# A transformer block on one Trainium2 core: other orders of operations at the edges of the two feed-forward blocks, and the last norm's weight taken into the last scaling

## The chip, the cores and the metric

The kernel runs on 1 core of one Trainium2 chip. The metric is the device time of one execution in microseconds (us). The core's engines work side by side, each through its own queue of instructions strictly in the order in which the program issues them: PE (TensorE, matmuls and transposes), DVE (VectorE), ACT (ScalarE), POOL (GpSimd) and SP (SyncE, which only starts transfers here). An instruction waits at the head of its queue until what it reads is there, and all behind it on that engine wait with it.

## The reference, cut

One block with fp32 weights and rows x of 512 x 1024, feed-forward width 2816:

```python
h = rms_norm(x, norm_ffn1);  x = x + 0.5 * swiglu(h, ffn1_gate, ffn1_up, ffn1_down)
h = rms_norm(x, norm_mix)    # RWKV7 time mix and sliding window attention on h @ w_in -> mixed
x = x + mixed @ w_out
h = rms_norm(x, norm_ffn2);  x = x + 0.5 * swiglu(h, ffn2_gate, ffn2_up, ffn2_down)
return rms_norm(x, norm_final)

def rms_norm(x, g):
    return x * rsqrt(mean(x * x, axis=-1) + 1e-5) * g
def swiglu(x, wg, wu, wd):
    return (silu(x @ wg) * (x @ wu)) @ wd
```

## The kernel before

Every fp32 product is made of three matmuls of rounded parts (`mm3w`, L679): high x high, low x high, high x low. So each operand exists as a high and a low part. ACT makes the high part by a copy (`high`, L160, names hia, hib for the weights of block a and b; L583 for the activations), DVE the low part by subtracting it (`low`, L169, loa and lob; L584).

The program has four stages: feed-forward block a, the mixer, `out_mix` (the product with w_out and its residual add), feed-forward block b with the final norm behind it. Names end in a or b by block.

A feed-forward block (`ffn`, L589) walks through *pieces* q of its weights, 128 x 1024 each, which `Stream` loads into rings of raw tiles (rawa0, rawa1, rawb), in the main on SP's queue; some pieces are sums of two blocks of weights, and for these POOL issues a second transfer that adds to the first (L128). Pieces 0 to 3 are *plain*: `plain_step` multiplies them with the block's operands into four accumulators Pa or Pb, one for each row tile t, six matmuls for each. Pieces 4 to 73 belong to a scheme of seven products for every 2 x 2 blocks, in the order M1 M2 M7 M6 M5 M3 M4 (accumulators X, Q, Y); M7 takes the difference s3 of two turned operands (L556). The 22 pieces after them are the down product, for the column half h = 0 and then h = 1. Step q of `ffn` issues, in this order: the loads of later pieces, the split of piece q + 2 (high and low part), the high part of piece q + 3, then `early` (work on operands), then the step of piece q itself, and last the *hidden turns* that are due, transposes of the gated values gta or gtb to hta or htb (L729).

The operands come from *turns*: `operand_turn` (L542) transposes four 128 x 128 blocks of row tile t, half h on PE into PSUM (xta, xtb; two such tiles exist), and DVE multiplies them by the norm's gain into xga or xgb (L549). `operand_split` then makes the two parts (ACT L583, DVE L584) into operands AaM, AaP (AbM, AbP). The norm's row scales do not enter the operands. They come from `row_squares` (ACT, L403, one square for each row tile) and `row_scales` (DVE L412, a pow on POOL into ms L414, DVE L416), and are first used by the gate gta, gtb (L656 on ACT, L657 on DVE).

In block a, `plain_step` of piece 0 turns rows 2 and 3 between its accumulators t=1 and t=2, and step 1 turns all four row tiles of half 1. For block b the turns lie in `out_mix` (L1563), whose step m multiplies w_out for row tile t = m % 4, column half m // 4, adds the result to xN (`out_add`, L1561, on DVE), and then issues turn m - 1. Behind turns 4 to 7 it squares a row tile and issues a store of it (`xd2`, on POOL's queue).

At the end, `down_post` (L760) adds a row tile's half to xN on DVE; `last_half` (L840) squares it on ACT and multiplies it by the final norm's weight nf on DVE (L847, into z), makes the sum of squares (L850) and the pow on POOL (L851); `last_row` (L853) scales z by the row's scale, half 0 on DVE and half 1 on ACT, and SP starts the stores.

Of the kernel before, what the change touches and what calls it, by code (L numbers as in the profile page):

```python
# [7 lines left out]
AF = mybir.ActivationFunctionType  # L8
ALU = mybir.AluOpType
AX = mybir.AxisListType  # L10
P = 128
S = 512
# [3 lines left out]
NF = F // P  # L16
# [16 lines left out]
P_OPERANDS = (("M1", "M2"), ("P21", "M4"))  # L33
# [12 lines left out]
             t="turn", te="evac_t", a="apply", ah="att_high", al="att_low", av="attn_values", vn="evac_vn", bp="bonus", bo="bonus_out",  # L46
# [136 lines left out]
class Net:  # L183
# [177 lines left out]
        self.operand_turn(self.xin[t], t, h, self.gain1)  # L361
        self.operand_split(P_OPERANDS[t // 2][h], t % 2)

    def start_step(self, q):

        if q == 1:
            for t in range(4):
                self.start_turn(t, 1)
        if q in (1, 2):
            for t in (2 * q - 2, 2 * q - 1):  # L370
                self.row_squares(self.xin[t], t)
        if q == 2:
            self.row_scales()

    def warm(self):

        nc = self.nc
        z = self.tile2("warm", (P, S), mybir.dt.bfloat16)
        nc.vector.memset(z, 0.0)
        a = self.small("warm_a", 1)  # L380
        nc.scalar.activation(a, z[:, 0:1], AF.Copy)
        pt = self.psum("warm_ps")
        for i in range(WARM):
            nc.tensor.matmul(pt, z[:, 0:P], z, start=True, stop=True)
# [204 lines left out]
    def ffn(self, tag):  # L589
        st = self.b if tag == "b" else self.a  # L590
        self.due = []
        self.banks = {}
        self.hT = {}
        self.temps = {}
        self.gtr = Ring(self.f, "gt" + tag, 8, F32, S)
        if tag == "a":
            self.xN = self.new_rows()
        n = len(st.pieces)
        for q in range(n):
            pc = st.pieces[q]  # L600
            st.loads(max(q + LOADS_D, min(q + LOADS, st.first_down)))
            st.split(q + LOW)
            st.high(q + HIGH)
            self.early(tag, st, q)
            if pc.kind == "p":
                self.plain_step(st, pc)
            elif pc.kind == "gu":
                self.gu_step(st, pc)
            else:
                self.down_step(st, pc)  # L610
            while self.due and self.due[0][0] <= q:
                self.due.pop(0)[1]()

    def early(self, tag, st, q):

        if tag == "a" and q < 8:
            self.start_step(q)
        if q in OPERANDS:
            self.operand_sum(OPERANDS[q])
            self.operand_split(OPERANDS[q])  # L620
        if tag == "a" and q == 6:
            self.vector_rows()
        if tag == "a" and q == 24:
            self.vectors()
        if tag == "a" and q == len(st.pieces) - 6:
            self.consts_mix()
        fd = st.first_down
        if q == fd + 2:
            if tag == "b":
                self.xN = self.new_rows()  # L630
            for t in range(4):
                self.nc.gpsimd.dma_start(self.xN[t], self.I["x"][0, t * P:(t + 1) * P] if tag == "a" else self.xd2[t])
        for i in {fd - 3: (0,), fd - 1: (1,)}.get(q, (q - fd + 2,) if q >= fd else ()):
            if i < len(KORDER):
                self.down_split(KORDER[i])

    def plain_step(self, st, pc):

        nc = self.nc
        if pc.idx == 0:  # L640
            self.banks["P"] = [self.acc(f"P{st.tag}{t}") for t in range(4)]
        bh, bl = st.parts[pc.q]
        for t in range(4):
            if st.tag == "a" and pc.idx == 0 and t == 2:
                for u in (2, 3):
                    self.start_turn(u, 0)
            hi, lo = self.A[P_OPERANDS[t // 2][pc.idx // 2]]
            ts = slice(t % 2 * P, t % 2 * P + P)
            for j in range(2):
                k = 2 * (pc.idx % 2) + j  # L650
                self.mm3w(self.banks["P"][t], hi[:, k, ts], lo[:, k, ts], bh[:, j], bl[:, j], pc.idx == 0 and j == 0, pc.idx == 3 and j == 1)
        if pc.idx == 3:
            for t, b in enumerate(self.banks.pop("P")):
                ms = self.ms[:, t:t + 1]
                g, h = self.gt(f"pg{st.tag}{t}")[:, :256], self.gt(f"ph{st.tag}{t}")[:, :256]
                nc.scalar.activation(g, b[:, 256:], AF.Silu, scale=ms)  # L656
                nc.vector.scalar_tensor_tensor(h, b[:, :256], ms, g, ALU.mult, ALU.mult)  # L657
                self.due.append((pc.q + 1 + t, lambda t=t, h=h: self.hidden_turn(st, 5, t, h, 256)))
# [80 lines left out]
    def down_step(self, st, pc):  # L739
        c, h, tag = pc.c, pc.idx, st.tag  # L740
        n = KORDER.index(c)
        last = n == NF // 2 - 1
        if n == 0:
            self.da = [self.acc(f"d{tag}{h}{t}") for t in range(4)]
        both = self.D[c]
        bh, bl = st.parts[pc.q]
        for t in range(4):
            ts = slice(t * P, t * P + P)
            for k in range(2):
                self.mm3w(self.da[t], both[:, 0, k, ts], both[:, 1, k, ts], bh[:, k], bl[:, k], n == 0 and k == 0, last and k == 1)  # L750
            if last:
                self.down_post(t, h)
                if h:
                    (self.last_a if tag == "a" else self.last_b)(t)
        if h:
            (self.tail_a if tag == "a" else self.tail_b)(n)
# [83 lines left out]
    def last_half(self, t, h):  # L840
        nc = self.nc
        if t not in self.z:
            self.z[t] = self.f.tile([P, D], F32, tag="z", name=f"z{t}", bufs=4)
        hs = slice(h * S, h * S + S)
        x, fs = self.xN[t][:, hs], self.fs[t]
        nc.scalar.activation(self.f.tile([P, D], F32, tag="sq", name=f"fsq{t}{h}", bufs=1)[:, :S], x, AF.Square, accum_out=fs[:, h:h + 1])
        nc.vector.tensor_tensor(self.z[t][:, hs], x, self.nf[:, hs], ALU.mult)  # L847
        if h:
            o = fs[:, 2:3]
            nc.vector.scalar_tensor_tensor(o, fs[:, 1:2], 1.0 / D, o, ALU.mult, ALU.add)  # L850
            nc.gpsimd.tensor_tensor(o, o, self.mhalf[:, 0:1], ALU.pow)  # L851

    def last_row(self, t):  # L853
        nc = self.nc
        z, o = self.z[t], self.fs[t][:, 2:3]
        for k in range(2):
            zh = z[:, k * S:(k + 1) * S]
            if k == 0:
                nc.vector.tensor_scalar(zh, zh, o, None, ALU.mult)
            else:  # L860
                nc.scalar.activation(zh, zh, AF.Copy, scale=o)
            nc.sync.dma_start(self.out[0, t * P:(t + 1) * P, k * S:(k + 1) * S], zh)

    def finish(self):
        self.last_row(3)
# [697 lines left out]
    def out_mix(self, next_gain):  # L1563
        st = self.b = self.stream("b")
        self.operands_begin("b")
        self.ss = self.small("ss_b", 8, "ss")
        self.xd2 = self.dram.tile([4, P, D], F32, name="x2_spill")
        c = self.col[next_gain]
        gain = self.vec[:, c:c + 8]
        def turn(m):  # L1570
            t, h = m % 4, m // 4
            self.operand_turn(self.xN[t], t, h, gain)
            self.operand_split(P_OPERANDS[t // 2][h], t % 2)
            if h:
                self.row_squares(self.xN[t], t)
                self.nc.gpsimd.dma_start(self.xd2[t], self.xN[t])
        w = {}
        for m in range(8):
            t, h = m % 4, m // 4
            if t == 0:  # L1580
                for i in (2 * h, 2 * h + 1):
                    w[i] = self.take(f"o1_{i}")
            ps = self.wo[m] = self.acc(f"wo1_{m}")
            for k in range(4):
                self.out_product(ps, self.mixed, w[2 * h + k // 2], t, k, k == 0, k == 3)
            if m < 2 and self.plan:
                self.want()
            self.out_add(m)
            if m < 4:
                st.loads(m + 1, self.nc.scalar)  # L1590
            if m:
                turn(m - 1)
            if m in (5, 6):
                st.split(m - 5)
        turn(7)
        self.row_scales()

def block(tc, I, out):
    with ExitStack() as ctx:
# [44 lines left out]
```

## Time and profile before

| | |
|---|---|
| median of 3 timed runs | 1011.6 us (1010.96 to 1013.06) |
| profiled execution, own time | 1009.71 us |
| its span in the profile | 1008.0 us |
| mean granted clock of PE | 0.985 |
| PE busy | 976.4 us (97%) |
| DVE busy | 653.3 us (65%) |
| ACT busy | 503.0 us (50%) |
| POOL busy | 87.7 us (9%) |

The times of the rows below are positions within the span. The profiled execution's own time is the span and 1.7 us around it. A granted clock of 1.00 is TensorE at 2.4 GHz, 0.50 at 1.2 GHz.

### The profile page before, as it was taken

What the parts mean: (1) busy time and instruction counts of PE and PEld (TensorE: products, weight loads), DVE (VectorE), ACT (ScalarE), POOL (GpSimd) and SP (SyncE); (2) the same over time, 40 slices, a digit from 0 to 9 for tenths busy, and PEclk for the clock granted to TensorE, in tenths of its full rate; (3) what the DMA queues carried; (4) which work ended last, traced back from release to release, by engine and by line L of the source; (5) the groups of instructions that cost most, each with busy time, mean ns of one, the idle gap of its engine ahead of it and who ended that gap; (6) DMA issues with size and microseconds to landing.
All of it is one profiled execution on the core that took longest, in us unless ns stands there. A gap on an engine that the chain in (4) does not pass through costs nothing.

```text
span 1008.0 us, 12969 instructions
## 1 busy us (share of the span) xinstructions
PE 976.4 (97%) x5041; PEld 794.5 (79%) x5041; DVE 653.3 (65%) x930; ACT 503.0 (50%) x777; POOL 87.7 (9%) x97
## 2 busy tenths in 40 slices
PE   6899999999999999999989999899999999999996
PEld 4678888888888886788876787687888888888885
DVE  4677676687532447689986797667767668753413
ACT  3555556546521318764467753355554654652302
POOL 1011100110000001110010030011110111000001
PEclk8999999999999999999999999999999999999998
DMA  9455945845323035223110254555594584533202
GB/s 314 104 140 127 230 100 156 191 101 210 125 95 93 7 83 163 62 85 74 42 33 22 74 158 163 174 144 143 122 236 107 145 197 105 199 125 124 64 1 84
DMA packets 83622, 124.09 MB, mean 123 GB/s; under 512 B 12773, under 2 KB 33321, under 8 KB 83561
## 3 DMA queue, kind: packets, MB, share of 16 engines
q1 hardware_dynamic: 67048, 89.17, 27.3%
q0 software_dynamic: 13856, 31.46, 15.8%
q10 hardware_dynamic: 2656, 2.63, 0.9%
q8 instruction: 39, 0.64, 0.3%
q14 instruction: 23, 0.18, 0.1%
HBM read 114.60 MB, written 6.29 MB: 120 GB/s over the span
## 4 chain that ended last, share of the span: by engine, by line
PE 87%; DVE 5%; ACT 3%; DMA 2%; issue 1%; POOL 0%; SPq 0%; POOLq 0%; ACTq 0%
PE da L681 4%; PE da L683 4%; PE da L682 4%; PE db L681 4%; PE db L683 4%; PE db L682 4%; PE Xa L683 4%; PE Xa L681 4%; PE Xa L682 4%; PE Xb L683 4%; PE Xb L681 3%; PE Xb L682 3%; PE Qa L683 2%; PE Qb L683 2%; PE Qa L681 2%; PE Qb L681 2%
## 5 line engine op out<-in xcount | busy, mean ns | idle before, releaser
L681 PE MATMUL da<-hia,dda 128*128 128x512 f32 x176 | 69.3, 394 | 0.0
L160 ACT ACTIVATE hib<-rawa1b 128x1024 fp32r<-128x1024 f32 x38 | 40.1, 1056 | 58.1 <-PE db L682 22.8
L681 PE MATMUL db<-hib,ddb 128*128 128x512 f32 x176 | 68.8, 391 | 0.0
L683 PE MATMUL da<-loa,dda 128*128 128x512 f32 x176 | 68.6, 390 | 0.0
L682 PE MATMUL da<-hia,dda 128*128 128x512 f32 x176 | 68.5, 389 | 0.0
L683 PE MATMUL db<-lob,ddb 128*128 128x512 f32 x176 | 68.5, 389 | 0.0
L682 PE MATMUL db<-hib,ddb 128*128 128x512 f32 x176 | 68.5, 389 | 0.0
L169 DVE TENSOR_TENSOR lob<-rawa0b,hib 128x1024 fp32r<-128x1024 f32 x38 | 46.4, 1220 | 29.5 <-PE db L683 21.7
L169 DVE TENSOR_TENSOR lob<-rawa1b,hib 128x1024 fp32r<-128x1024 f32 x38 | 46.4, 1220 | 29.5 <-PE db L683 22.7
L160 ACT ACTIVATE hia<-rawa1a 128x1024 fp32r<-128x1024 f32 x38 | 40.1, 1055 | 50.3 <-DMA rawa1a<-in_ffn_gate_dram 18.3
L681 PE MATMUL Xa<-hia,AaM 128*128 128x512 f32 x160 | 64.3, 402 | 0.0
L683 PE MATMUL Xa<-loa,AaM 128*128 128x512 f32 x160 | 63.2, 395 | 0.3 <-DVE loa L169 0.3
L682 PE MATMUL Xa<-hia,AaM 128*128 128x512 f32 x160 | 63.2, 395 | 0.0
L683 PE MATMUL Xb<-lob,AbM 128*128 128x512 f32 x160 | 62.5, 391 | 0.6 <-DVE lob L169 0.6
L681 PE MATMUL Xb<-hib,AbM 128*128 128x512 f32 x160 | 63.1, 395 | 0.0
L682 PE MATMUL Xb<-hib,AbM 128*128 128x512 f32 x160 | 62.3, 389 | 0.0
L169 DVE TENSOR_TENSOR loa<-rawa0a,hia 128x1024 fp32r<-128x1024 f32 x38 | 46.3, 1220 | 23.5 <-PE da L683 14.6
L169 DVE TENSOR_TENSOR loa<-rawa1a,hia 128x1024 fp32r<-128x1024 f32 x38 | 46.4, 1220 | 16.1 <-PE da L683 8.8
L160 ACT ACTIVATE hib<-rawa0b 128x1024 fp32r<-128x1024 f32 x38 | 40.1, 1056 | 23.8 <-PE db L682 15.6
L160 ACT ACTIVATE hia<-rawa0a 128x1024 fp32r<-128x1024 f32 x38 | 40.1, 1055 | 18.0 <-PE da L682 11.2
L683 PEld LDWEIGHTS da<-loa,dda 128*128 128x128 f32 x176 | 33.0, 188 | 7.0
L683 PEld LDWEIGHTS db<-lob,ddb 128*128 128x128 f32 x176 | 33.0, 188 | 7.0
(460 smaller groups left out, 2527.9 us busy)
## 6 DMA issues: line engine op xcount, KB each, us to landing
rawa0a<-in_w_in_dram SPq DMA_DIRECT2D x16, 512.0 KB
rawa0a<-in_ffn_down_dram SPq DMA_DIRECT2D x11, 512.0 KB
rawa1a<-in_ffn_down_dram SPq DMA_DIRECT2D x11, 512.0 KB
rawa0b<-in_ffn_down_dram SPq DMA_DIRECT2D x11, 512.0 KB
rawa1b<-in_ffn_down_dram SPq DMA_DIRECT2D x11, 512.0 KB
rawba<-in_ffn_up_dram SPq DMA_DIRECT2D x10, 512.0 KB
rawba<-in_ffn_gate_dram SPq DMA_DIRECT2D x10, 512.0 KB
rawa0a<-in_ffn_gate_dram POOLq DMA_DIRECT2D x10, 512.0 KB, 6.0
```

The costliest lines, as they stand in the source:

```text
L160: self.nc.scalar.activation(hi, raw, AF.Copy)
L169: self.nc.vector.tensor_tensor(lo, raw, hi.bitcast(F32), ALU.subtract)
L681: mm(ps, ah, bh, start=first, stop=False, skip_group_check=True)
L682: mm(ps, al, bh, start=False, stop=False, skip_group_check=True)
L683: mm(ps, ah, bl, start=False, stop=last, skip_group_check=True)
```

## The change

Four places change; the matmuls are the same in kind and number.

1. Block a, piece 0: its `plain_step` is issued ahead of the split of piece 2 and the high part of piece 3. In it, rows 2 and 3 are turned between t=0 and t=1, both turns first and then both splits. `start_step` is dissolved into `early`.
2. `out_mix` and block b: turn 7 is issued inside the first plain step of block b, between t=1 and t=2 (12 matmuls into it). The splits of pieces 0 and 1 come one step m earlier. The four squares move from the turns to steps q = 1 and 2 of block b, and the row scales to q = 2. On POOL the pow for ms thereby stands behind the additions of pieces 8 and 9 (L128), one of which also comes ahead of the last xN store.
3. Block b, down product, h = 1: the last two pieces are taken together, so that an accumulator is done every 12 matmuls at the end, where it was every 6.
4. `last_half` no longer multiplies half 1 by nf; `last_row` scales half 0 on ACT, and half 1 on DVE by one fused operation with the row's scale and nf. DVE has 883 rows in place of 888.

```diff
     def ffn(self, tag):
...
             st.loads(max(q + LOADS_D, min(q + LOADS, st.first_down)))
+            if tag == "a" and q == 0:
+                self.plain_step(st, pc)
             st.split(q + LOW)
             st.high(q + HIGH)
             self.early(tag, st, q)
             if pc.kind == "p":
-                self.plain_step(st, pc)
+                if tag == "b" or q:
+                    self.plain_step(st, pc)
...
     def early(self, tag, st, q):
-        if tag == "a" and q < 8:
-            self.start_step(q)
+        if tag == "a" and q == 1:
+            for t in range(4):
+                self.start_turn(t, 1)
+        if q in (1, 2):
+            for t in (2 * q - 2, 2 * q - 1):
+                self.row_squares((self.xin if tag == "a" else self.xN)[t], t)
+        if q == 2:
+            self.row_scales()
...
         for t in range(4):
-            if st.tag == "a" and pc.idx == 0 and t == 2:
+            if pc.idx == 0 and t == 1 and st.tag == "a":
                 for u in (2, 3):
-                    self.start_turn(u, 0)
+                    self.operand_turn(self.xin[u], u, 0, self.gain1)
+                for u in (2, 3):
+                    self.operand_split(P_OPERANDS[1][0], u % 2)
+            if pc.idx == 0 and t == 2 and st.tag == "b":
+                self.out_turn(7)
...
+        paired = tag == "b" and h == 1
+        pieces = [pc]
+        if paired and n == NF // 2 - 2:
+            self.held_piece = pc
+            pieces = []
+        elif paired and last:
+            pieces = [self.held_piece, pc]
+        for t in range(4) if pieces else ():
             ts = slice(t * P, t * P + P)
-            for k in range(2):
...
+            for x in pieces:
+                both = self.D[x.c]
+                bh, bl = st.parts[x.q]
+                for k in range(2):
...
-        nc.vector.tensor_tensor(self.z[t][:, hs], x, self.nf[:, hs], ALU.mult)
         if h:
...
+        else:
+            nc.vector.tensor_tensor(self.z[t][:, hs], x, self.nf[:, hs], ALU.mult)
...
             if k == 0:
-                nc.vector.tensor_scalar(zh, zh, o, None, ALU.mult)
+                nc.scalar.activation(z[:, hs], z[:, hs], AF.Copy, scale=o)
             else:
-                nc.scalar.activation(zh, zh, AF.Copy, scale=o)
...
+                nc.vector.scalar_tensor_tensor(z[:, hs], self.xN[t][:, hs], o, self.nf[:, hs], ALU.mult, ALU.mult)
...
             if m:
-                turn(m - 1)
-            if m in (5, 6):
-                st.split(m - 5)
-        turn(7)
-        self.row_scales()
+                self.out_turn(m - 1)
+            if m in (4, 5):
+                st.split(m - 4)
+
+    def out_turn(self, m):
+        t, h = m % 4, m // 4
+        self.operand_turn(self.xN[t], t, h, self.gain2)
+        self.operand_split(P_OPERANDS[t // 2][h], t % 2)
+        if h:
+            self.nc.gpsimd.dma_start(self.xd2[t], self.xN[t])
```

The order on DVE at the start of block a, before. (xga_137 holds turned rows 0 and 1, xga_138 rows 2 and 3 until the last row shown, which belongs to half 1 again; AaP is the operand of rows 2 and 3; the first low part is that of piece 1, the next those of pieces 2 and 3.)

```order
L169 TENSOR_TENSOR loa<-rawa1a,hia 128x1024
L169 TENSOR_TENSOR loa<-rawa0a,hia 128x1024
L549 TENSOR_TENSOR xga_138<-xta_191,pack_106 128x4x128
L584 TENSOR_TENSOR AaP_197<-xga_138,AaP_197 128x4x128
L549 TENSOR_TENSOR xga_138<-xta_200,pack_106 128x4x128
L584 TENSOR_TENSOR AaP_197<-xga_138,AaP_197 128x4x128
L169 TENSOR_TENSOR loa<-rawa1a,hia 128x1024
```

The same place after the change, where the source lines have shifted by some 11:

```order
L538 TENSOR_TENSOR xga_138<-xta_180,pack_106 128x4x128
L538 TENSOR_TENSOR xga_138<-xta_186,pack_106 128x4x128
L573 TENSOR_TENSOR AaP_192<-xga_138,AaP_192 128x4x128 x2
L169 TENSOR_TENSOR loa<-rawa1a,hia 128x1024
L169 TENSOR_TENSOR loa<-rawa0a,hia 128x1024
L169 TENSOR_TENSOR loa<-rawa1a,hia 128x1024
L538 TENSOR_TENSOR xga_137<-xta_224,pack_106 128x4x128
```

The two turns and their splits moved from behind the low part of piece 2 to ahead of the low part of piece 1.

The order on DVE from the fifth add of `out_mix` on (wo_4 to wo_7 are the accumulators of steps m = 4 to 7), before. The two low parts are those of pieces 0 and 1 of block b.

```order
L1561 TENSOR_TENSOR xN_4453<-wo_4_4904,xN_4453 128x512
L549 TENSOR_TENSOR xgb_4794<-xtb_4918,pack_106 128x4x128
L584 TENSOR_TENSOR AbP_4901<-xgb_4794,AbP_4901 128x4x128
L1561 TENSOR_TENSOR xN_4453<-wo_5_4926,xN_4453 128x512
L549 TENSOR_TENSOR xgb_4793<-xtb_4940,pack_106 128x4x128
L584 TENSOR_TENSOR AbM_4946<-xgb_4793,AbM_4946 128x4x128
L169 TENSOR_TENSOR lob<-rawa0b,hib 128x1024
L1561 TENSOR_TENSOR xN_4454<-wo_6_4956,xN_4454 128x512
L549 TENSOR_TENSOR xgb_4793<-xtb_4970,pack_106 128x4x128
L584 TENSOR_TENSOR AbM_4946<-xgb_4793,AbM_4946 128x4x128
L169 TENSOR_TENSOR lob<-rawa1b,hib 128x1024
L1561 TENSOR_TENSOR xN_4454<-wo_7_4983,xN_4454 128x512
```

The same place after:

```order
L1573 TENSOR_TENSOR xN_4453<-wo_4_4904,xN_4453 128x512
L538 TENSOR_TENSOR xgb_4794<-xtb_4918,pack_106 128x4x128
L573 TENSOR_TENSOR AbP_4901<-xgb_4794,AbP_4901 128x4x128
L169 TENSOR_TENSOR lob<-rawa0b,hib 128x1024
L1573 TENSOR_TENSOR xN_4453<-wo_5_4930,xN_4453 128x512
L538 TENSOR_TENSOR xgb_4793<-xtb_4944,pack_106 128x4x128
L573 TENSOR_TENSOR AbM_4950<-xgb_4793,AbM_4950 128x4x128
L169 TENSOR_TENSOR lob<-rawa1b,hib 128x1024
L1573 TENSOR_TENSOR xN_4454<-wo_6_4956,xN_4454 128x512
L538 TENSOR_TENSOR xgb_4793<-xtb_4970,pack_106 128x4x128
L573 TENSOR_TENSOR AbM_4950<-xgb_4793,AbM_4950 128x4x128
L1573 TENSOR_TENSOR xN_4454<-wo_7_4979,xN_4454 128x512
```

The low part of piece 0 moved ahead of the sixth add, that of piece 1 ahead of the seventh; the eighth add (wo_7) follows the parts of turn 5 (AbM) directly.

The order on DVE behind the last down products, the last two row tiles, before (db are the accumulators, fs the rows' sums and scales):

```order
L760 SCALAR_TENSOR_TENSOR xN_6573<-db_6848,xN_6573 128x512
L847 TENSOR_TENSOR z_6971<-xN_6573,nf 128x512
L850 SCALAR_TENSOR_TENSOR fs_6878<-fs_6878 128x1
L859 TENSOR_SCALAR z_6939<-z_6939,fs_6877 128x512
L760 SCALAR_TENSOR_TENSOR xN_6573<-db_6849,xN_6573 128x512
L847 TENSOR_TENSOR z_7003<-xN_6573,nf 128x512
L850 SCALAR_TENSOR_TENSOR fs_6879<-fs_6879 128x1
L859 TENSOR_SCALAR z_6971<-z_6971,fs_6878 128x512
L859 TENSOR_SCALAR z_7003<-z_7003,fs_6879 128x512
```

and after:

```order
L771 SCALAR_TENSOR_TENSOR xN_6573<-db_6848,xN_6573 128x512
L860 SCALAR_TENSOR_TENSOR fs_6878<-fs_6878 128x1
L873 SCALAR_TENSOR_TENSOR z_6939<-xN_6572,fs_6877,nf 128x512
L771 SCALAR_TENSOR_TENSOR xN_6573<-db_6849,xN_6573 128x512
L860 SCALAR_TENSOR_TENSOR fs_6879<-fs_6879 128x1
L873 SCALAR_TENSOR_TENSOR z_6971<-xN_6573,fs_6878,nf 128x512
L873 SCALAR_TENSOR_TENSOR z_7003<-xN_6573,fs_6879,nf 128x512
```

The multiply by nf (L847) is gone from between the adds, and the last scalings are fused operations that read xN and nf.

## Rows read from the trace of the kernel before

**Rows 1.** PE's waits, whole span: us in total, times, longest us.
```profile
PE hta L729 <- DVE gta L657: 4.3, 1, 4.3
PE xtb L547 <- DVE xN L1561: 4.2, 1, 4.2
PE Pa L681 <- ACT AaP L583: 3.7, 1, 3.7
```

**Rows 2.** Windows: us; PE, PEld, DVE, ACT, POOL busy; PE clock; DMA share; GB/s.
```profile
8.05:12.35 4.30, 3.78 (x10) 2.67 (x11) 3.35 (x4) 1.58 (x2) 0.00 (x0) 0.60 1.07 385
652.50:657.25 4.75, 4.75 (x13) 3.89 (x14) 2.70 (x5) 3.86 (x7) 0.76 (x2) 0.50 0.86 251
```

**Rows 3.** Timeline of PE, block a: start, us, instruction, [idle before <- releaser].
```profile
11.18 0.63 PE L681 MATMUL Pa<-hia,AaM 128*128 128x512 f32 x1
...
22.74 1.91 PE L547 MATMUL xta<-pack,xN 128*128 128x128 f32 x16
...
48.05 0.69 PE L729 MATMUL hta<-pack,gta 128*128 128x128 f32 x2 [4.32 <-DVE gta L657]
```

**Rows 4.** Timelines of ACT and DVE, block a.
```profile
14.16 1.06 ACT L160 ACTIVATE hia<-rawa0a 128x1024 fp32r<-128x1024 f32 x1 [2.69 <-DMA rawa0a<-in_ffn_gate_dram]
...
23.37 0.69 DVE L549 TENSOR_TENSOR xga<-xta,pack 128x512 f32<-128x512 f32 x1 [1.79 <-PE xta L547]
...
37.42 1.22 DVE L556 TENSOR_TENSOR s3a<-xga,xga 128x1024 f32<-128x1024 f32 x1
```

**Rows 5.** Timeline of PE, end of out_mix and start of block b.
```profile
647.74 0.60 PE L547 MATMUL xtb<-pack,xN 128*128 128x128 f32 x4
679.74 0.38 PE L729 MATMUL htb<-pack,gtb 128*128 128x128 f32 x2
697.02 0.50 PE L683 MATMUL Xb<-lob,AbM 128*128 128x512 f32 x1 [0.64 <-DVE lob L169]
```

**Rows 6.** Timeline of DVE, the same stretch.
```profile
646.66 0.68 DVE L1561 TENSOR_TENSOR xN<-wo,xN 128x512 f32<-128x512 f32 x1
647.26 0.68 DVE L549 TENSOR_TENSOR xgb<-xtb,pack 128x512 f32<-128x512 f32 x1
648.63 0.69 DVE L584 TENSOR_TENSOR AbM<-xgb,AbM 128x512 fp32r<-128x512 f32 x1 [0.70 <-ACT AbM L583]
650.62 1.22 DVE L169 TENSOR_TENSOR lob<-rawa1b,hib 128x1024 fp32r<-128x1024 f32 x1 [1.29 <-ACT hib L160]
651.76 0.68 DVE L1561 TENSOR_TENSOR xN<-wo,xN 128x512 f32<-128x512 f32 x1
...
658.20 1.22 DVE L169 TENSOR_TENSOR lob<-rawa0b,hib 128x1024 fp32r<-128x1024 f32 x1
...
662.10 1.22 DVE L556 TENSOR_TENSOR s3b<-xgb,xgb 128x1024 f32<-128x1024 f32 x1
...
678.12 2.35 DVE L169 TENSOR_TENSOR lob<-rawbb,hib 128x1024 fp32r<-128x1024 f32 x2
```

**Rows 7.** Timeline of ACT, the same stretch.
```profile
639.65 0.63 ACT L583 ACTIVATE AbP<-xgb 128x512 fp32r<-128x512 f32 x1 [2.50 <-DVE xgb L549]
...
655.60 1.04 ACT L403 ACTIVATE sq3None<-xN 128x1024 f32<-128x1024 f32 x1
```

**Rows 8.** Timelines of PE, DVE and ACT, the end.
```profile
989.71 0.39 PE L683 MATMUL db<-lob,ddb 128*128 128x512 f32 x1
...
998.55 0.39 PE L683 MATMUL db<-lob,ddb 128*128 128x512 f32 x1
1000.47 0.69 DVE L760 SCALAR_TENSOR_TENSOR xN<-db,xN 128x512 f32<-128x512 f32 x1
...
1003.00 0.49 DVE L859 TENSOR_SCALAR z<-z,fs 128x512 f32<-128x512 f32 x1 [0.43 <-POOL fs L851]
1003.00 0.72 ACT L861 ACTIVATE z<-z,fs 128x512 f32<-128x512 f32 x1 [0.41 <-POOL fs L851]
```

**Rows 9.** DMA view, 600 to 680: queue, count, KB each, us to landing.
```profile
rawa1b<-in_ffn_gate_dram POOLq DMA_DIRECT2D x1, 512.0 KB, 11.1
```

More of the change, by code (lines that the diff above doesn't have):

```diff
@@ L362, in start_turn @@
         self.operand_split(P_OPERANDS[t // 2][h], t % 2)
[L364 to L372, printed above, removed]
-            self.row_scales()
     def warm(self):
@@ L744, in down_step @@
             self.da = [self.acc(f"d{tag}{h}{t}") for t in range(4)]
-        both = self.D[c]
-        bh, bl = st.parts[pc.q]
-        for t in range(4):
-            ts = slice(t * P, t * P + P)
-            for k in range(2):
-                self.mm3w(self.da[t], both[:, 0, k, ts], both[:, 1, k, ts], bh[:, k], bl[:, k], n == 0 and k == 0, last and k == 1)
+        paired = tag == "b" and h == 1
[6 more added lines that the diff above has]
+        for t in range(4) if pieces else ():
+            ts = slice(t * P, t * P + P)
+            for x in pieces:
+                both = self.D[x.c]
+                bh, bl = st.parts[x.q]
+                for k in range(2):
+                    self.mm3w(self.da[t], both[:, 0, k, ts], both[:, 1, k, ts], bh[:, k], bl[:, k], n == 0 and k == 0,
+                              last and x is pc and k == 1)
             if last:
@@ L856, in last_row @@
         for k in range(2):
-            zh = z[:, k * S:(k + 1) * S]
+            hs = slice(k * S, (k + 1) * S)
             if k == 0:
-                nc.vector.tensor_scalar(zh, zh, o, None, ALU.mult)
+                nc.scalar.activation(z[:, hs], z[:, hs], AF.Copy, scale=o)
             else:
-                nc.scalar.activation(zh, zh, AF.Copy, scale=o)
-            nc.sync.dma_start(self.out[0, t * P:(t + 1) * P, k * S:(k + 1) * S], zh)
+                nc.vector.scalar_tensor_tensor(z[:, hs], self.xN[t][:, hs], o, self.nf[:, hs], ALU.mult, ALU.mult)
+            nc.sync.dma_start(self.out[0, t * P:(t + 1) * P, hs], z[:, hs])
     def finish(self):
@@ L1568, in out_mix @@
         c = self.col[next_gain]
[L1569 to L1576, printed above, removed]
+        self.gain2 = self.vec[:, c:c + 8]
         w = {}
@@ L1591, in out_mix @@
             if m:
-                turn(m - 1)
-            if m in (5, 6):
-                st.split(m - 5)
-        turn(7)
-        self.row_scales()
+                self.out_turn(m - 1)
[7 more added lines that the diff above has]
+            self.nc.gpsimd.dma_start(self.xd2[t], self.xN[t])
 def block(tc, I, out):
```

## The prediction, made before the changed kernel was run

> **What bounds the kernel now.** I read the page's busy shares first: PE is busy 976.4 of 1008.0 us, DVE 65%, ACT 50%, POOL 9%. So only what PE loses at its waits, at a low clock, and behind its last matmul can be won. The view of PE's waits comes next [rows 1]: three stalls of about 4 us stand out from all others (the fourth is 1.6). All three are at the edges of the feed-forward blocks: Pa (t=2 of the first plain piece waits for its operand), hta (the first hidden transposes of block a), xtb (turn 7 waits for the residual add of out_mix). The windows then show what a stall costs beyond itself [rows 2]: behind the xtb stall PE's granted clock is 0.50 for 4.75 us, the lower of its two levels (1.2 of 2.4 GHz). The timelines tell what each stall waits for, and the end of DVE's and ACT's timeline shows what runs after PE's last matmul.
>
> **Start.** In the kernel before, DVE makes the low part of piece 2 before it turns rows 2 and 3, and that piece lands only when ACT begins its high part at 14.16 [rows 4]. DVE's multiply for row 2 therefore comes at 16.4, the operand at 17.8 (PE waits 3.7), PE reaches the turns of half 1 at 22.74 [rows 3], and DVE multiplies the first of them at 23.37 [rows 4]. From there on the chain is DVE's and ACT's until the gate gta, for which PE waits until 48.05 [rows 3]; whatever 23.37 gains, 48.05 gains.
> After the change the transposes of rows 2 and 3 follow the sixth Pa product, at about 11.2 [rows 3], and no piece is ahead of them. With 0.6 to 0.7 us per 512-wide and 1.14 per 1024-wide DVE operation (starts 646.66, 647.26 and 650.62, 651.76 in [rows 6]) DVE does both multiplies by 13.6, both low parts by 14.9. ACT's high parts of pieces 1, 2, 3 then start at about 14.15, 15.1 and 16.05 (0.95 apart), the low parts at 15.2, 16.35 and 17.5, and the first half-1 multiply at 18.65. That is 23.37 - 18.65 = **4.7 us**. PE has the piece done at about 17.0 if the clock is full after the transposes (18 products at 0.227: 39 steps from 989.71 to 998.55 in [rows 8]) and so hides behind DVE. The wait at hta stays as long as it was. If the three low parts were 0.2 us less or more each, the term would be 5.3 or 4.1; the low end of the range comes from the clock, below.
>
> **Middle.** What PE can win is the idle 4.16 of [rows 1] and the half-clock stretch, 4.75 x 0.5 = 2.4, thus 6.5 together. The turn that waited is now issued after 12 products of FFN b's first plain piece, 12 x 0.227 = 2.7 after PE ends its previous turn (647.74 in [rows 5] plus 0.4), so it needs the eighth add (add 7, counted from 0) at 650.9. Before, that add starts at 651.76 [rows 6]: two squares (1.04 each on ACT) and two high parts stood in the way of DVE's low parts, which waited 1.29 for ACT. I rebuild the new order from ACT's operand split at 639.65 [rows 7]: the high part of piece 0 at 640.2, its low part on DVE at 641.3 (a high part is 1.06 in [rows 4]), add 5 at 642.4, turn 4 and its split to 644.4 (turn to low part takes 647.26 to 648.63 = 1.37 in [rows 6]), low part of piece 1 at 645.3, add 6 at 646.5, turn 5 and its split, add 7 at 649.0, done at 649.7. PE needs it at 650.9, so the stall goes, with 1.2 to spare, and without an idle of that size the clock has no cause to fall.
> What is late next? The squares are not removed, they move behind the turns, and the row scales with them. DVE goes on: turns 6 and 7 at 649.6 and 653.1, low parts of pieces 2, 3, 4 at 652.0, 655.1, 656.2. ACT has the four squares at 655.3, 656.4, 658.4 and 659.4, between the high parts of pieces 4 and 5. Behind the last square the scales take 2.6 (655.60 in [rows 7] to 658.20 in [rows 6]), so s3b starts at 662.0, where it starts now (662.10 in [rows 6]), while PE is 6.5 earlier. All of DVE's slack there is spent. From s3 to the first hidden transposes block a takes 48.05 - 37.42 = 10.6 [rows 3, 4]: ready at 672.7. PE needs htb at 679.74 - 6.5 = 673.2 [rows 5], so it just makes it. The next handoff is the low part for M6, where PE waits 0.64 at 697.02 [rows 5], which is DVE's low part begun 1.2 earlier. DVE runs 17.6 from the low parts at 678.12 [rows 6] to that one; about 1.4 of this is waiting for PE's own products, which come earlier. From 673.75 that makes 16.2 + 1.2: ready at 691.2. PE comes at 697.02 - 0.64 - 6.7 = 689.7, so it waits 1.5 instead of 0.64, and about 0.7 of the 6.5 is given back. The term is **5.8 us**; its bounds are 6.5 (all won) and 4.4 (1.4 more given back, as if none of PE's earlier products helped DVE).
>
> **End.** After PE's last matmul at 998.55 DVE still has a queue: its work per row tile is about 2.0 (add 0.72, multiply by the norm's weight 0.8, scale column, scaling), while PE delivers a tile every 6 products, 1.36. So the last add starts at 1000.47, 1.9 after the matmul [rows 8]. Two edits remove this: tiles now come 12 products, 2.72, apart, and the weight's multiply leaves the chain. The last add starts at about 998.8, and the same 2.5 to the last scaling (1003.00 - 1000.47) brings that to 1001.35. DVE's scaling is then the fused form, 0.69 as the add's in [rows 8], against 0.49; ACT's other half takes 0.72 as before. The gain is 1.65 less 0.15 to 0.2, **1.5 us** (1.3 if the fused form delays both stores by its full 0.2 and 0.1 more, 1.8 if nothing is lost). Pairing two pieces adds no product and needs the parts of one piece longer; no load is still due there, so it costs nothing.
>
> **Sum.** 4.7 + 5.8 + 1.5 = 12.0 off the profiled execution's own 1009.7: 997.7. The median of the timed runs is 1.9 above the profiled one, so I forecast **999.6**. The bounds of the terms alone (4.1 to 5.3, 4.4 to 6.5, 1.3 to 1.8) give 9.8 to 13.6, thus 998.0 to 1001.8.
>
> **Rivals.** (1) *DVE and ACT become the bound of FFN b's first group.* The margins at htb (0.5) and M6 (-1.5) come out of my rebuilt queue and hang on some ten pitches. If s3b is 2 us later than I think, PE waits 1.5 at htb and has 3.5 lost by M6, 2.9 more than before, and an idle like that has cost the clock here: 2.4 more. For it: hta in block a does stall 4.3 with the same DVE work behind the same plain pieces [rows 3]. Against it: block b has its operands of half 0 ready before the pieces begin. The middle term is then 6.5 - 2.9 - 2.4 = 1.2, the total 7.4: 1004.2.
> (2) *The clock rises later at the start.* PE's first products ran at granted 0.60 in 8.05 to 12.35 [rows 2], the release falling inside it or at its end. Those products come before the moved turns, and in the new order the short turns stand where long products stood. If PE stays at half clock through the piece, its 18 products from 12.7 take 18 x 0.45 (twice 0.227) = 8.2, and the first half-1 turn follows at 20.9; with half a microsecond for it the multiply at 21.4 makes the start term 2.0, the total 9.3: 1002.3. The Trainium skill, TensorE: Matmul & The Clock Gate, Part 1 (What's actually happening), says the throttled state is the default, that activity releases it, and that the number of slow matmuls at a kernel's start differs from run to run. By that rule the start term is anywhere between 2.0 and 4.7 in any one run; the trace agrees as to the slow start (0.60), and one profile can't show the spread.
> (3) *Slower.* The pow of the row scales stands on POOL now behind the gate additions of pieces 8 and 9 (before it stood ahead of both), and each of these waits until SP's load into that buffer has landed. I put POOL free at 653 against a need at 660.6, with SP's load for piece 9 issued at about 646.6. The landing of such a transfer on POOL's own queue takes 11.1 [rows 9]; if SP's took 23, the scales would be at 670.7, 10 late, s3b, htb and PE with them, and with the clock's 2.4 this eats the 12.0. From there it is slower. The rows show nothing near 23.
> (4) *It does nothing measurable:* DVE's first-group chain in b gives back all of the middle and the clock all but 2 of the start.
>
> **Chances.** Forecast 0.60, rival 1 0.20, rival 2 0.12, slower 0.04, same 0.04. About 0.2%, 2 us, is what a measurement of this kernel can tell from no change; all of the first three are beyond it, so faster is 0.91 with a little put to same. The range goes from 996.5 (the best of each term and 1.5 for the timed median's own scatter, 1011.0 to 1013.1) to 1005.0 (rival 1 with its clock loss).
>
> **What would show it.** Start: no stall at Pa for AaP, first half-1 multiply near 18.7, hta near 43.4 with a stall of 4 to 5 left. Middle: no stall at xtb, no 0.50 stretch behind it, s3b near 662 minus the 4.7 of the start, a stall of 1 to 2 at the M6 low part, none at htb. End: last add 0.3 behind PE's last matmul, span ending about 8 behind that matmul instead of 9.4. I am wrong if htb stalls, if the pow waits on POOL, or if PE's clock stays low through the first piece.

## The result, and the profile after

The changed kernel takes 1001.25 us (median of 4 runs, 999.24 to 1002.43), the kernel before 1011.28 (4 runs): ratio 0.9895, 95% interval 0.9868 to 0.9922. The forecast was 999.6, so 12.0 off was forecast and 10.0 came. In more executions later the changed kernel stood at 1001.21 (5 runs), ratio 0.9897 (0.9880 to 0.9914).

PE's waits in the changed kernel (us in total, times, longest), which answer to [rows 1]:

```profile
PE hta L731 <- DVE gta L659: 4.6, 1, 4.6
PE xta L536 <- DMA xN<-in_x_dram: 2.5, 1, 2.5
PE rstd_ps L411 <- POOL ms L403: 1.6, 1, 1.6
PE avn L1429 <- ACT held L924: 1.4, 1, 1.4
PE Xb L685 <- DVE lob L169: 1.3, 2, 0.7
```

The stalls at Pa and xtb are gone, hta has kept its own (4.6, before 4.3), and the low parts of block b have 1.3 where they had 0.6. The waits at rstd_ps and avn lie outside the edited places and are as before (1.6 and 1.5). The one at xta is the first load of x; it is the same code in both kernels and took 1.4 before:

```profile
PE xta L547 <- DMA xN<-in_x_dram: 1.4, 1, 1.4
```

The start, on PE and DVE (to be read against [rows 3, 4]):

```profile
11.79 1.91 PE L536 MATMUL xta<-pack,xN 128*128 128x128 f32 x8
12.88 0.69 DVE L538 TENSOR_TENSOR xga<-xta,pack 128x512 f32<-128x512 f32 x1 [1.33 <-PE xta L536]
14.34 1.48 DVE L573 TENSOR_TENSOR AaP<-xga,AaP 128x512 fp32r<-128x512 f32 x2
19.49 0.68 DVE L538 TENSOR_TENSOR xga<-xta,pack 128x512 f32<-128x512 f32 x1
31.96 0.17 DVE L401 TENSOR_SCALAR ss_a<-ss_a 128x4 f32<-128x4 f32 x1 [3.28 <-ACT sq3None L392]
33.45 0.17 DVE L405 TENSOR_SCALAR nms<-ms 128x4 f32<-128x4 f32 x1 [1.33 <-POOL ms L403]
33.53 1.22 DVE L545 TENSOR_TENSOR s3a<-xga,xga 128x1024 f32<-128x1024 f32 x1
44.16 0.69 PE L731 MATMUL hta<-pack,gta 128*128 128x128 f32 x2 [4.60 <-DVE gta L659]
```

The turns of rows 2 and 3 come before any low part of a later piece; the first half-1 multiply starts at 19.49 (23.37 before) and hta at 44.16 (48.05).

The seam of out_mix and block b, on DVE and PE ([rows 5, 6]), and POOL's pow:

```profile
648.85 0.68 DVE L1573 TENSOR_TENSOR xN<-wo,xN 128x512 f32<-128x512 f32 x1
650.73 0.60 PE L536 MATMUL xtb<-pack,xN 128*128 128x128 f32 x4
660.71 0.17 DVE L401 TENSOR_SCALAR ss_b<-ss_b 128x4 f32<-128x4 f32 x1 [3.38 <-ACT sq3None L392]
660.97 1.04 POOL L403 TENSOR_TENSOR ms<-ss_b,pack 128x4 f32<-128x4 f32 x1 [8.88 <-DVE ss_b L401]
662.12 1.22 DVE L545 TENSOR_TENSOR s3b<-xgb,xgb 128x1024 f32<-128x1024 f32 x1
672.98 0.38 PE L731 MATMUL htb<-pack,gtb 128*128 128x128 f32 x2
```

Add 7 is done before PE's twelve products are, so turn 7 runs without an idle; in the window view of this stretch (columns as in [rows 2]) the clock stays up:

```profile
652.00:656.00 4.00, 4.00 (x20) 3.27 (x19) 3.30 (x4) 3.06 (x4) 0.09 (x1) 1.00 1.09 313
```

The end ([rows 8]):

```profile
992.71 0.39 PE L685 MATMUL db<-lob,ddb 128*128 128x512 f32 x1
993.13 0.69 DVE L771 SCALAR_TENSOR_TENSOR xN<-db,xN 128x512 f32<-128x512 f32 x1 [0.35 <-PE db L685]
995.93 0.75 DVE L873 SCALAR_TENSOR_TENSOR z<-xN,fs,nf 128x512 f32<-128x512 f32 x1 [0.44 <-POOL fs L861]
995.93 0.72 ACT L871 ACTIVATE z<-z,fs 128x512 f32<-128x512 f32 x1 [0.68 <-POOL fs L861]
```

Counted from the start of PE's last matmul, the last add comes 0.4 behind it (1.9 before), and the span of 1000.7 ends 8.0 behind it (9.4 before).

**Where the rest went.** The same instruction stands in both timelines, so the difference of its two starts tells how much has been won up to there. For the profiled execution of the changed kernel it is -4.6 at DVE's 500.58 (in the mixer), but -0.2 at 629.33, where the first turn of out_mix is multiplied: 4.4 of the 4.6 of the start are lost in the mixer, in code that the change doesn't touch. No wait grows there. The windows show the clock. First before, then after (columns as in [rows 2]):

```profile
560.00:564.00 4.00, 4.00 (x38) 3.51 (x35) 3.80 (x14) 3.14 (x7) 0.00 (x0) 1.00 0.02 4
564.00:568.00 4.00, 4.00 (x35) 2.53 (x33) 1.43 (x7) 3.01 (x12) 0.00 (x0) 1.00 0.01 2
572.00:576.00 4.00, 4.00 (x28) 3.00 (x28) 2.65 (x13) 2.04 (x9) 0.00 (x0) 1.00 0.40 77
```

```profile
560.00:564.00 4.00, 4.00 (x32) 2.97 (x31) 1.46 (x5) 3.67 (x13) 0.00 (x0) 0.89 0.01 2
564.00:568.00 4.00, 4.00 (x40) 2.58 (x39) 2.81 (x13) 1.57 (x5) 0.00 (x0) 0.68 0.00 0
572.00:576.00 4.00, 4.00 (x24) 2.81 (x24) 3.30 (x13) 2.12 (x7) 0.00 (x0) 0.67 0.81 227
```

PE is busy in all six windows, with short products of the attention and the time mix; only its granted clock differs. This is 3.1 of the 4.4. The other 1.3 is lost earlier, between 526 and 534, where the clock is low in both kernels, but longer in the changed one. First before, then after:

```profile
524.00:528.00 4.00, 2.58 (x26) 2.14 (x27) 3.52 (x16) 3.71 (x14) 0.00 (x0) 0.95 0.00 0
528.00:532.00 4.00, 4.00 (x16) 1.99 (x12) 2.87 (x12) 1.50 (x4) 0.00 (x0) 0.62 0.02 4
```

```profile
524.00:528.00 4.00, 4.00 (x8) 1.76 (x8) 2.35 (x9) 1.95 (x7) 0.00 (x0) 0.50 0.02 4
528.00:532.00 4.00, 4.00 (x34) 2.70 (x33) 1.58 (x4) 2.69 (x10) 0.00 (x0) 0.87 0.00 0
```

### The profile page after: what moved, and what is told of

The parts are those of the page before. It is cut to its first block, busy times and chain, and to the rows that moved or that the text cites. A ratio compares the mean times of both kernels' runs of the same rounds, so it can differ in the third digit from the quotient of the medians.

```text
span 1000.7 us, 12967 instructions
## 1 busy us (share of the span) xinstructions
PE 976.9 (98%) x5041; PEld 794.6 (79%) x5041; DVE 651.7 (65%) x926; ACT 502.9 (50%) x777; POOL 88.5 (9%) x97
## 4 chain that ended last, share of the span: by engine, by line
PE 85%; DVE 6%; ACT 4%; issue 2%; DMA 1%; POOL 1%; SPq 0%; POOLq 0%; ACTq 0%; DVEq 0%
PE da L685 4%; PE da L683 4%; PE db L685 4%; PE db L683 4%; PE da L684 4%; PE db L684 4%; PE Xa L685 4%; PE Xa L683 4%; PE Xa L684 4%; PE Xb L685 3%; PE Xb L683 3%; PE Xb L684 3%; PE Qb L685 2%; PE Qa L685 2%; PE Qa L683 2%
```

## The experiments

For each profiled execution the positions minus those of the kernel before (us): in the mixer (DVE, 500.58 before), at the first turn of out_mix (629.33), in block b (AbM of M5, 682.74), and the tail from the start of PE's last matmul to the span's end. The last two columns are differences of these: what the mixer lost, what the middle won.

| kernel | mixer | out_mix | block b | tail | mixer lost | middle won |
|---|---|---|---|---|---|---|
| before | 0 | 0 | 0 | 9.4 | | |
| changed | -4.6 | -0.2 | -5.9 | 8.0 | 4.4 | 5.6 |
| changed, again | -4.6 | -2.5 | -8.2 | 8.0 | 2.2 | 5.7 |
| start alone | -5.0 | -0.5 | -1.4 | 9.4 | 4.4 | 0.8 |
| middle alone | 0.8 | 0.8 | -4.9 | 9.4 | 0.0 | 5.6 |
| end alone | 1.7 | 2.2 | 2.2 | 8.0 | 0.5 | 0.0 |
| pairing alone | 0.4 | 0.4 | 0.5 | 8.0 | 0.0 | -0.1 |
| squares back | -5.6 | -1.4 | -6.4 | 8.0 | 4.3 | 5.1 |
| turn 7 back | -5.0 | -5.0 | -9.9 | 8.0 | 0.0 | 4.9 |
| scales split | -5.8 | -5.2 | -11.8 | 8.0 | 0.6 | 6.6 |
| scales split, 0.9 later | -6.1 | -4.5 | -11.0 | 8.0 | 1.6 | 6.6 |
| gates first | -8.3 | -4.4 | -8.2 | 8.0 | 3.9 | 3.8 |
| changed, 1.6 later | -3.0 | -2.3 | -7.9 | 8.0 | 0.7 | 5.6 |
| changed, 3.2 later | -1.6 | -1.1 | -6.8 | 8.0 | 0.5 | 5.7 |

**The parts alone.** The start alone is part 1 of the diff on the kernel before, the middle alone part 2, the end alone parts 3 and 4.

> Only the edit of block a's first piece on the kernel before (part 1). Theory: the first half-1 multiply comes 3.9 earlier and everything to the mixer 4.6 earlier, as in the changed kernel; what the mixer then loses to PE's clock differs between executions, so the median is 3 to 5 us below the kernel before, and in the profile the positions of out_mix stand 0 to 4.6 us earlier. Rival A: an earlier mixer always falls worse with the clock, so the gain ends there and the median is within 1 us of before.

Measured 1007.95 (9 runs) against 1010.93 (21 runs of before, 1008.60 to 1014.93): ratio 0.9961 (0.9947 to 0.9975). The seam in the mixer is 5.0 earlier, the median 3.0. Eight of the nine runs lie between 1007.0 and 1008.3 and one at 1004.9. So rival A holds in part: the gain arrives in the mixer, and a good part of it usually ends there. PE's mean granted clock goes with it: 0.985 or 0.986 in the eight runs, 0.987 in the ninth. The middle won 0.8 in this profile with no edit there: the stall at xtb is 4.16 as before, but the clock behind it was back sooner (0.63 in 652 to 656 where before has 0.50).

> Only the edits of out_mix and block b's first steps on the kernel before (part 2). Theory: no stall at xtb, no half-clock stretch behind it, htb 6 to 7 us earlier against the start of out_mix, 0.5 to 1 given back at low parts for M6: median 5 to 6.5 us below before. Rival B: part of the 5.6 seen in the changed kernel came from what the start edit left behind (another clock state), and alone it gives under 4.

Measured 1005.72 (6 runs), ratio 0.9947 (0.9930 to 0.9963): 5.2 below before, and 5.6 in the trace without the start edit. Rival B falls.

> Only the pairing of the last two down pieces and the norm's weight in the last scaling, on the kernel before (parts 3 and 4). Theory: last add 0.3 us behind PE's last matmul, span ends 8.0 behind that matmul in place of 9.4: median 1.0 to 2.0 below before. Rival C: the pairing costs PE a wait elsewhere, and the gain is under 0.7.

Measured 1009.31 (12 runs), ratio 0.9983 (0.9973 to 0.9994): 1.6 below. Rival C falls: the tail is 8.0. This run also shows how far unchanged code can move: its block a, the same as before, ran 1.7 later, with a granted clock of 0.61 in 16 to 24 where that of before is 0.79.

> Only the pairing of the last two down pieces on the kernel before (part 3), the norm's weight still multiplied on DVE. Theory: row tiles come 2.7 apart and DVE needs 2.0 for each, so the last add starts 0.3 behind PE's last matmul as with both edits, but the multiply (0.8) is still ahead of the scale: the span ends 7.9 to 8.5 behind the last matmul, so nearly all of the gain is the pairing's. Rival: the multiply is on the chain and half of the gain is lost, 8.7 or more.

Measured 1008.82 (one run). The end of its timeline:

```profile
999.13 0.39 PE L683 MATMUL db<-lob,ddb 128*128 128x512 f32 x1
999.56 0.69 DVE L769 SCALAR_TENSOR_TENSOR xN<-db,xN 128x512 f32<-128x512 f32 x1 [0.62 <-PE db L683]
1000.28 0.69 DVE L856 TENSOR_TENSOR z<-xN,nf 128x512 f32<-128x512 f32 x1
1001.10 0.16 DVE L859 SCALAR_TENSOR_TENSOR fs<-fs 128x1 f32<-128x1 f32 x1
1002.09 0.48 DVE L868 TENSOR_SCALAR z<-z,fs 128x512 f32<-128x512 f32 x1 [0.43 <-POOL fs L860]
```

The span of 1007.1 ends 8.0 behind the last matmul, as with both edits. The pairing does all of it. DVE's multiply (1000.28) runs while ACT squares the same tile, so the sum of squares is not held up, and taking the multiply out shortens nothing there. From the last add to the last scaling it is 2.53 here and before, but 2.80 in the changed kernel (993.13 to 995.93). The difference is POOL's pow, here first in this run and then in the changed kernel:

```profile
1001.34 0.72 POOL L860 TENSOR_TENSOR fs<-fs,pack 128x1 f32<-128x1 f32 x1 [2.00 <-DVE fs L859]
994.91 0.98 POOL L861 TENSOR_TENSOR fs<-fs,pack 128x1 f32<-128x1 f32 x1 [1.73 <-DVE fs L860]
```

Behind the last scaling the span ends 0.2 sooner in the changed kernel (4.8 in place of 5.0), so the fused form costs some 0.27 and gives 0.2 back: it is worth nothing.

**What made the middle.** Two of its moves are undone, one at a time, in the changed kernel.

```diff
     def out_turn(self, m):
...
         if h:
+            self.row_squares(self.xN[t], t)
             self.nc.gpsimd.dma_start(self.xd2[t], self.xN[t])
```

> The changed kernel with the four squares of block b back in the turns of out_mix (the scales stay at step 2, turn 7 stays in the plain step). Theory: two squares (1.04 each) stand again ahead of high parts on ACT, add 7 comes 2.1 later, 0.9 after PE wants it: a stall of about 1 at xtb; s3b comes 2 to 4 us earlier than 662, which takes the waits at M6's low parts (1.3) away: within 1 us of the changed kernel. Rival: the squares were the stall; with them back PE stalls 3 to 4 at xtb and the clock falls behind it, 4 to 6 us slower.

Measured 1001.89 (4 runs), ratio 0.9906 (0.9892 to 0.9920). PE waits 0.4 at xtb, s3b starts at 659.84, the middle wins 5.1 in place of 5.6. The theory holds in the time (0.7 above the changed kernel's 1001.2): the squares were not the stall by themselves. Its sizes were off: the stall is 0.4 and not 1, half of the 2.3 that s3b comes earlier than in the changed kernel is an out_mix that starts earlier here, and a wait of 0.7 at a low part is left.

```diff
             if m in (4, 5):
                 st.split(m - 4)
+        self.out_turn(7)
...
-            if pc.idx == 0 and t == 2 and st.tag == "b":
-                self.out_turn(7)
```

> The changed kernel with turn 7 back at the end of out_mix (squares and scales stay late, splits one step earlier). Theory: add 7 is ready at 649.5 in the changed kernel's positions and PE, with no products in between, wants it at 647.9: a stall of 1.6 to 1.8 at xtb in place of 4.2, the clock stays high, 1 to 2 us slower than the changed kernel. Rival: any stall there costs the clock as well, 4 us slower.

Measured 1001.63 (4 runs), ratio 0.9908 (0.9894 to 0.9923): 0.4 above the changed kernel, which these runs cannot tell from nothing. Two waits of PE:

```profile
PE xtb L536 <- DVE xN L1571: 1.5, 1, 1.5
PE Xb L683 <- DVE lob L169: 0.7, 1, 0.7
```

The stall is 1.5, the clock stays up behind it, and the middle still wins 4.9. The windows behind the two stalls (columns as in [rows 2]), first turn 7 back (stall until 644.81), then squares back (until 646.90):

```profile
644.00:648.00 4.00, 3.19 (x16) 2.73 (x17) 2.64 (x5) 1.20 (x3) 2.69 (x3) 1.00 1.00 325
648.00:652.00 4.00, 4.00 (x22) 3.25 (x21) 2.58 (x4) 3.08 (x7) 2.88 (x3) 1.00 0.98 307
```

Of the 5.6, then, turn 7's place is worth 0.7 and the squares' 0.6 when each alone is undone; either one, with the splits a step earlier, leaves a stall of 0.4 or 1.5, behind which the clock stayed up. The third move, the splits of pieces 0 and 1 a step earlier, stands in both kernels. No run has it alone or takes it back, so how much of the 5.6 is its own is not shown.

**What the mixer loses.** Is it the place where its work falls against the clock, or chance? Extra products whose result nothing reads delay the mixer:

```diff
+        if tag == "a" and h == 0 and n == 2:
+            both, bh = self.D[c], st.parts[pc.q][0]
+            pt = self.tp("extra", (P, S))
+            for i in range(7):
+                self.nc.tensor.matmul(pt, both[:, 0, 0, 0:P], bh[:, 0], start=True, stop=True)
```

> The changed kernel once more, for more executions. Theory (position): the mixer's two stretches of low clock near 525 and 565 come because its work starts 4.6 to 5.0 us earlier against the clock's own beat, so most executions have them, the median stays at 1001 and a few lie 3 lower. Rival (chance): they come to any kernel in any execution alike; then the median falls to about 999, or the times split evenly.

> The changed kernel with 7 extra products (7 x 0.227 = 1.6 us) whose result nothing reads, in block a's down product. Theory (position): the mixer then starts 3.0 earlier than in the kernel before, not 4.6, and if the low-clock stretch near 565 (3.1) depends on where it starts it can go: between 1.5 us faster and 1.6 slower than the changed kernel. Rival (chance): 1.6 slower, with the same spread.

> The changed kernel with 14 extra products (3.2 us) at the same place as the 7 before. Theory (position): its mixer starts 1.4 earlier than in the kernel before, the low-clock stretch near 565 is gone, and the median lies within 1 us of the changed kernel, 1001 to 1002. Rival (chance): 3.2 slower than the changed kernel, 1004.4.

> The kernel with the scales split, with 4 extra products (0.9 us) in block a's down product, so that its mixer starts 4.9 earlier than in the kernel before, where the start edit alone put it, and not 5.8. Theory (position): the low-clock stretch near 565 comes back, 3 to 4 us slower than without the delay. Rival (chance): 0.9 slower.

The changed kernel again: 1001.21 (5 runs, 999.09 to 1002.20). The median stayed at 1001, where chance as I put it asked for 999; but the same program lost 4.4 in one profiled execution and 2.2 in the other, so it is not position alone. With 7 extra products 1001.05 (4 runs), ratio 0.9899 (0.9883 to 0.9915): not slower, but 1.6 lies within what the intervals leave open. With 14: 1005.03 (6 runs), ratio 0.9930 (0.9916 to 0.9944), which is 3.8 slower than the changed kernel, near the 3.2 of chance and against position. Its profiled execution lost 0.5 and took 1001.50; four of its six runs lie at 1005.0 to 1005.3, 3.5 above that. The split kernel with 4 extra products: 997.86 (4 runs), ratio 0.9864 (0.9844 to 0.9883), 1.4 slower than without, nearer to 0.9 than to 3 or 4; its profiled execution does not bear on position, as its mixer began 6.1 early and not the 4.9 that were meant. And turn 7 back began its mixer 5.0 earlier, as the start alone did, and lost nothing. So position as I put it, the mixer's start against the kernel before, falls: of the eight profiled executions whose mixer began over 4 us early six lost 1.6 to 4.4 and two 0.0 and 0.6, of the six others (before among them, and the two with 7 and 14 extra products) none lost over 0.7.

It is not uneven chance either; the kept traces sort it. In all 14 profiled executions the granted clock falls to 0.50 early in the mixer, the first time at 517.6 to 528.4, in or behind an idle of PE of 1.4 to 1.5. Counted from the mixer's row (500.58 before) of the same execution, the place of this first fall goes with the loss:

| from the mixer's row to the clock's first fall, us | executions | mixer lost |
|---|---|---|
| 24.0 | changed, again | 2.2 |
| 24.1 to 24.8 | end alone; changed, 3.2 later; scales split; changed, 1.6 later | 0.5 to 0.7 |
| 25.3 to 26.2 | gates first; squares back; start alone; changed | 3.9 to 4.4 |
| 26.9 | scales split, 0.9 later | 1.6 |
| 27.0 to 27.2 | middle alone; before; turn 7 back; pairing alone | 0.0 |

The changed kernel and the start alone have the same place (26.2) and the same loss (4.4). So what the mixer loses goes with the place in its own work at which the clock falls in that execution, and two executions of one program can differ in it (26.2 and 24.0). This was read from the profiles afterwards; no run set the place. Single timed runs 3 to 4 above the rest occur with before, too (1014.55 and 1014.93 of 21). Why the start edit brings the costly place so often stays open.

**A version beyond both.** hta still stalled 4.6 in the changed kernel. There DVE waits 3.28 for the last square and 1.33 for the pow ahead of s3a (31.96 and 33.45 above); in block b the row at 660.71 shows the same. The next kernel takes s3 and its split first:

```diff
+        if q == 3:
+            self.scales_first()
+        if q in OPERANDS:
+            self.operand_sum(OPERANDS[q])
+            self.operand_split(OPERANDS[q])
         if q in (1, 2):
             for t in (2 * q - 2, 2 * q - 1):
                 self.row_squares((self.xin if tag == "a" else self.xN)[t], t)
-        if q == 2:
-            self.row_scales()
-        if q in OPERANDS:
-            self.operand_sum(OPERANDS[q])
-            self.operand_split(OPERANDS[q])
+        if q == 3:
+            self.scales_last()
```

(`scales_first` is the first operation and the pow of `row_scales`, `scales_last` its last operation.)

> The changed kernel with one more move, in both blocks: s3 and its split ahead of squares 2 and 3, the first scale operation and the pow one step later, the negated scales behind M6's operand. Theory: the stall at hta in block a is DVE waiting 3.3 for the last square and 1.3 for the pow ahead of s3; without this s3a starts 4 to 5 us earlier, the hta stall of 4.6 falls under 1 and the half-clock stretch behind it (2.4) goes, and in block b the waits at low parts (1.3) go: median 6 to 8 us below the changed kernel, about 994. Rival D: the stall is ACT's (table load and gate behind M6's operand) and moves less than 2 us.

Measured 996.50 (5 runs, 994.82 to 997.63), ratio to before 0.9850 (0.9830 to 0.9871), 4.7 below the changed kernel's median and less than the 6 to 8 expected. Two rows of its trace, and three of ACT:

```profile
28.28 1.22 DVE L555 TENSOR_TENSOR s3a<-xga,xga 128x1024 f32<-128x1024 f32 x1
38.98 0.79 PE L695 MATMUL Xa<-hia,AaM 128*128 128x512 f32 x1 [3.09 <-DVE gta L671]
35.57 1.06 ACT L579 ACTIVATE AaM<-xga 128x1024 fp32r<-128x1024 f32 x1 [1.86 <-DVE xga L558]
36.64 1.28 ACT L670 ACT_TABLE_LOAD   x1
37.94 1.57 ACT L670 ACTIVATE gta<-Pa,ms 128x256 f32<-128x256 f32 x4
```

s3a is 5.2 earlier, but the stall of 4.6 became one of 3.1 a little further on: the first products into Xa wait for an accumulator that the gates set free, and these stand on ACT behind M6's high part and the table load. Rival D holds for that remainder. In block b the middle wins 6.6 in place of 5.6, which is all of the 6.5 that the prediction put at stake there.

The last kernel, against the split one, loads the table early and takes M6's operand behind the gates:

```diff
-OPERANDS = {2: "M7", 3: "M6", 5: "M5", 7: "M3"}
+OPERANDS = {2: "M7", 4: "M6", 5: "M5", 7: "M3"}
...
+        if q == 2:
+            self.nc.scalar.activation(self.small(f"silu_{tag}", 1), self.ss[:, 0:1], AF.Silu)
```

> The kernel with the scales split, with two more moves in both blocks: a small Silu behind square 3, so that ACT loads its table there and not ahead of the gate, and M6's sum and split one step later, behind the gates. Theory: in block a PE waits 3.1 at Xa for an accumulator that the gates set free, which stand behind M6's high part (1.0) and the table load (1.3) on ACT; without these the wait falls to about 1 and the half-clock stretch behind it goes: 2 to 4 us below the split kernel, about 993. Rival: M6's low part comes too late for its pieces and PE waits there: no gain.

Measured 1000.06 (4 runs), ratio 0.9884 (0.9870 to 0.9899): slower than the split kernel. Its waits:

```profile
PE Xa L699 <- DVE loa L169: 2.6, 2, 1.8
PE Xb L699 <- DVE lob L169: 2.5, 2, 1.8
...
PE Xa L697 <- DVE gta L673: 1.0, 1, 1.0
```

The wait for the accumulator fell from 3.1 to 1.0, and block a ran 2.5 earlier than in the split kernel. But the sums and the low part of M6 now stand on DVE ahead of a low part of the weights that PE needs, and in block b, which had no such stall to win, that costs 2.8 of the middle; the rival holds there. The edit's own places thus come out 0.3 behind (2.8 less 2.5). The rest of the 3.6 between the medians is, in the profiles, the mixer: it lost 3.9 here and 0.6 in the split kernel, with the clock's fall at another place (25.3 and 24.3 in the table above).

## Why the prediction was right, point by point

- **Start, 4.7 forecast:** 3.9 at the multiply (19.49), and 3.9 at hta, so what the one gains the other gains, as forecast. That the gain is 4.6 behind hta is luck: the low-clock stretch there was shorter (0.53 in 44 to 48 and 1.00 in 48 to 52, before 0.50 in 48 to 52), and the prediction has no term for that. The moved transposes began 0.6 later than I put them (11.79) and took 1.9 for the eight, ACT's high parts began 0.9 later (15.00), and the multiply came 0.8 later. A part of this is the execution and not the sum: PE waited 2.5 for the load of x, before 1.4. In the nine other profiled executions with this start the multiply comes at 18.00 to 19.18, which is 4.2 to 5.4 won; and where block a has this edit alone (changed twice, start alone, squares back, turn 7 back), the mixer's row is 4.6 to 5.6 early. Rival 2, the clock low through the whole piece, did not come in this execution; 18 products fit between 13.35 and 17.7.
- **Middle, 5.8 forecast:** 5.6 measured, 5.6 alone. Add 7 was put at 649.0 and came at 648.85 while the mixer had left only 0.2 of the start; s3b was put at 662.0 and came at 662.12; the waits at the low parts, put at 1.5, are 1.3. (The prediction takes PE as 6.7 earlier at this one point and 6.5 everywhere else; with 6.5 the wait is 1.3 and the 0.7 given back follows. Its 673.75, from where it counts to M6's low part, stands there without its working; the low parts meant start at 673.77.) Rival 1 did not come: htb has no wait. Nor did the slower one: the pow runs 0.26 behind its operand's start (660.97, 660.71).
- **End, 1.5 forecast:** 1.44 (9.45 to 8.01). The sum was right, its parts were not: the add comes 0.42 behind the matmul (put at 0.25), the scaling 2.80 behind the add (put at 2.5), and the span ends 4.8 behind the scaling's start, where 5.0 and 0.15 to 0.2 more was put; the misses cancel. That both edits are needed was wrong, too: the pairing alone gives it.
- **Sum, 12.0 forecast:** 11.7 at the three places (4.64 + 5.64 + 1.44), 7.3 between the two profiled executions (1009.71 to 1002.43), 10.0 in the medians. The step that failed is the silent one in it: that what is won at the start travels unchanged to the end. The mixer took 4.4 of it in one execution, 2.2 in another, and on the median of the start alone 2.0 (5.0 less 3.0). Nor does it hold in the mixer that the clock has no cause to fall without an idle of the size of 4.16: it fell three times there, with no idle of PE over 1.5. That the forecast is only 1.7 off is partly luck. It adds 1.9 because the median before lay 1.9 above the profiled execution; in the changed kernel the median lies 1.2 below it (1001.25, 1002.43), and these 3.1 hide most of what the mixer took.
- **The range** held, and so did the narrower bounds of the terms alone (998.0 to 1001.8), by the same luck: neither had a term for the mixer.

## What to carry to other kernels

Where an engine is busy 97% of the time, look for the few stalls at the seams and for what the clock costs behind them; then, for each, rebuild the waiting engine's queue row by row in its new order with measured pitches. That gave the middle to 0.2 us here, and the start to 0.8 in this execution. Before a gain is carried to the end of a span, ask which later stretch has a clock that comes and goes, and take several executions of either kernel to see its spread. And two orders that each cure a stall (turn 7 later, squares later) need not add: undone alone, either cost 0.6 or 0.7 of 5.6. A move that stays in every run, as the earlier splits here, has no price.

## What the runs showed of the hardware

The granted clock can fall where PE's records show no idle: 0.68 in 564 to 568 of the changed kernel, with PE busy throughout with short products. The Trainium skill, TensorE: Matmul & The Clock Gate, Part 1 (A second HAM failure mode: psum-queue depth-cycling), tells of a kernel in which many small gaps between groups of matmuls let the clock swing; the records here, whose ends are modelled, show no such gaps in that stretch, so they neither bear it out nor refute it.

The length of a stall does not by itself tell what follows. One of 1.5 us between long products (turn 7 back) left the clock up. One of 4.16 was followed by 0.50 for 4.75 us [rows 2]:

```profile
652.50 1.12 PE L547 MATMUL xtb<-pack,xN 128*128 128x128 f32 x4 [4.16 <-DVE xN L1561]
```

And in the mixer, amid short products, the clock fell to 0.50 in or behind an idle of 1.4 to 1.5, in all 14 profiled executions.

POOL's pow on a tile of 128 x 1 took 0.98 to 0.99 in all ten profiled executions with the fused scaling and 0.72 to 0.73 in the four without it, the first of the four row tiles apart (0.57 or 0.58 in all). In the ten, DVE's fused scaling of the row tile before runs beside it (994.75 to 995.50 in the changed kernel); that this is the cause is not shown.
